# Up projection of a block-algorithm FFN on one core: two channel tiles interleaved, product by product

## Chip, cores, metric

The kernel runs on one core of one Trainium2 chip. The metric is the time of one execution in microseconds (us) of device time, lower is better; where several executions were timed, their median counts. PE is TensorE, DVE is VectorE, ACT is ScalarE, POOL is GpSimd, and SP is the engine whose queue issues nearly all DMAs.

## What is computed

One layer: a token mixer (DeltaNet and grid pooling, not touched here), then a gated FFN with a three-tap convolution over the sequence, all in float32. The change is inside the FFN, for 1024 tokens, D = 1024 and 2816 = 22 x 128 hidden channels:

```python
def conv_glu_ffn(h, w_up, conv_w, w_down):
    gate, up = jnp.split(h @ w_up, 2, axis=-1)
    return (jax.nn.silu(depthwise_conv(gate, conv_w)) * up) @ w_down
```

## The kernel before

Every float32 product is made of three matmuls: each operand is split into a rounded part (`h`) and the rest (`l`), and h·h, l·h and h·l are added up in PSUM. ACT makes the rounded part with a CAST, DVE the rest with a TENSOR_TENSOR.

The up projection works on 22 channel tiles f = 0..21. For one tile, the weights of the gate half and the up half (each 1024 x 128) and the activations (1024 x 1024) are taken as a 2 x 2 block product, which a Strassen-like scheme computes with seven block products instead of eight. Each of the seven is 4 k-blocks x 3 matmuls = 12 matmuls of 128x128 weights and 512 columns. Table `PROD` (line 1463) gives each product its weight block, its activation block and its PSUM bank:

| product p | moving operand | PSUM | what its eviction does |
|---|---|---|---|
| 1 | b11 | pa (X) | ACT copies it to `t1` |
| 6 | T2 | pb (Y) | DVE: gate half 1 = PSUM + t1 (`graw`) |
| 2 | b21 | pa (X, added to 1) | ACT copies it to gate half 0 (`graw`) |
| 7 | T3 | pb (Y, added to 6) | DVE: up half 1 = PSUM + t1 (`upx`) |
| 5 | T1 | pc (Z) | DVE: up half 1 += PSUM |
| 4 | T4 | pb (Y, added to 7) | DVE: up half 0 = PSUM + t1 |
| 3 | B22 | pc (Z, added to 5) | DVE: gate half 1 += PSUM |

Since products share banks, `NEEDS = {2: 1, 7: 6, 4: 7, 3: 5}` (line 1591) makes product 2 wait for the eviction of 1, 7 for that of 6, 4 for that of 7, and 3 for that of 5. `stream_up` (1593) walks through `SEQ` (1465 to 1467); there, tile after tile, the order is 1, 6, 2, 7, 5, 4, 3. The first tiles are special: products of tiles 0 and 1 alternate, and products 1 and 2 of tile 2 are drawn ahead.

The other work of a tile:

- `prep` (1480) loads four weight blocks (tiles `a11`, `a21`, `a22`, `a12`, 256 KB each, eight buffers) and a fifth (`st2`, one buffer), and POOL forms one sum and three differences of them in place.
- `stream_split` (1536) makes the weight halves `wqh` (ACT) and `wql` (DVE) of each product, four buffers each (`NWQ`), in the order of `SEQ`.
- `up_out` (1621) is the eviction. `graw` and `upx` come from one ring of four buffers (`gu`, 1659).
- `gate` (1662) does the convolution on DVE (one TENSOR_SCALAR, two SCALAR_TENSOR_TENSOR), SiLU on ACT, the product with `upx` on DVE and the store `gd`; its result lies in `hf[4 + f % 4]`, where `hf` is a block of eight 128x1024 slots.
- Once per pair of tiles: `sums_S` (1698) makes four sums and differences for the down projection from the two results and stores them (`sd`); `sums_T` (1710) loads two row blocks of `w_down`, makes four differences and stores them (`td`). The two use `hf[0:2]` and `hf[2:4]`. All eleven `sums_T` are done by 972 us.

The engines run their own queues in order. The order in a queue is not that of the Python text: the generators are merged by priority (`Streams`, 128) and the framework then places the instructions. Then follows the down projection (`stream_down`, 1758): 924 matmuls in seven passes.

Of the kernel before, what the change touches and what calls it, by code (L numbers as in the profile page):

```python
# [25 lines left out]
NF = 22  # L26
# [101 lines left out]
class Streams:  # L128
# [7 lines left out]
    def spawn(self, gen, prio):  # L136
        self.active.append([prio, max(self.now, self.clock.end), gen, None, 0])

    def signal(self, name):
        self.events[name] = max(self.now, self.clock.end)  # L140
# [42 lines left out]
def kernel(ctx: ExitStack, tc: tile.TileContext, I, out):  # L183
    nc = tc.nc
    clock = Clock()
    V, S, G, TE, SY = [Engine(clock, n, e) for n, e in (("DVE", nc.vector), ("ACT", nc.scalar), ("POOL", nc.gpsimd),
                                                        ("PE", nc.tensor), ("SP", nc.sync))]
# [1121 lines left out]
    W = {}  # L1309
# [154 lines left out]
            5: ("S1", "T1", "Z"), 6: ("S2", "T2", "Y"), 7: ("S3", "T3", "Y")}  # L1464
    SEQ = [(f, p) for p in (1, 2) for f in (0, 1)] + [(2, 1), (2, 2)]
    SEQ += [(f, p) for p in (6, 7, 5, 4, 3) for f in (0, 1)]
    SEQ += [(f, p) for f in range(2, NF) for p in (1, 6, 2, 7, 5, 4, 3) if f > 2 or p > 2]
    NWQ, NST = 4, 8
    half = (slice(0, 512), slice(512, 1024))
    NJ = NF // 2  # L1470
    CH = [f // 2 + NJ * (f % 2) for f in range(NF)]
    A, wq, up, bank = {}, {}, {}, {}
# [148 lines left out]
    def up_out(f, p, ps):  # L1621

        yield (ps,)
        if p == 1:
            up[f, "t1"] = fT.tile([P, 512], F32, name="t1", bufs=2)
            S.copy(up[f, "t1"], ps)
        else:
            for e in {6: (1,), 5: (7,), 4: (1,), 3: (6,)}.get(p, ()):
                yield f"E{f}{e}"
            if (f, "g") not in up:  # L1630
                yield "FB"
                if f > 1:
                    yield f"g{f - 2}"
            if (f, "g") not in up:
                up[f, "g"] = gu("graw")
                G.memset(up[f, "g"][:, 0:1], 0.0)
                G.memset(up[f, "g"][:, T + 1:T + 2], 0.0)
                up[f, "u"] = gu("upx")
            g, u, t1 = up[f, "g"], up[f, "u"], up[f, "t1"]
            g0, g1 = [g[:, 1 + h.start:1 + h.stop] for h in half]  # L1640
            u0, u1 = [u[:, h] for h in half]
            if p == 2:
                S.copy(g0, ps)
            elif p == 6:
                V.tensor_tensor(g1, ps, t1, ALU.add)
            elif p == 7:
                V.tensor_tensor(u1, ps, t1, ALU.add)
            elif p == 5:
                V.tensor_tensor(u1, ps, u1, ALU.add)
            elif p == 4:  # L1650
                V.tensor_tensor(u0, ps, t1, ALU.add)
            else:
                V.tensor_tensor(g1, ps, g1, ALU.add)
        yield
        signal(f"E{f}{p}")
        if p == 3:
            spawn(gate(f), 3)

    def gu(name):
        return fb.tile([P, T + 2], F32, name=name, tag="gu", bufs=4)  # L1660

    def gate(f):
        yield "TD"
        yield f"E{f}4"
        cw = sm[:, SM_FCONV + 3 * CH[f]:SM_FCONV + 3 * CH[f] + 3]
        rw, u, sg = up[f, "g"], up[f, "u"], W["hf"][:, 4 + f % 4, :]
        V.tensor_scalar(sg, rw[:, 0:T], cw[:, 0:1], None, ALU.mult)
        yield
        V.scalar_tensor_tensor(sg, rw[:, 1:T + 1], cw[:, 1:2], sg, ALU.mult, ALU.add)
        yield  # L1670
        V.scalar_tensor_tensor(sg, rw[:, 2:T + 2], cw[:, 2:3], sg, ALU.mult, ALU.add)
        yield
        S.activation(sg, sg, AF.Silu)
        yield
        V.tensor_tensor(sg, u[:, 0:T], sg, ALU.mult)
        yield
        dma(out=gd[f], in_=sg)
        signal(f"g{f}")
        if f % 2:
            spawn(sums_S(f // 2), 4)  # L1680
        else:
            spawn(sums_T(f // 2), 5)
        yield
# [13 lines left out]

    def sums_S(j):

        (a11, a21), (a12, a22) = [[W["hf"][:, 4 + f % 4, h] for h in half] for f in (2 * j, 2 * j + 1)]  # L1700
        s1, s2, s3, s4 = [blocks(0)[:, i] for i in range(4)]
        for x, y, z, op in ((s1, a21, a22, ALU.add), (s2, s1, a11, ALU.subtract), (s3, a11, a21, ALU.subtract),
                            (s4, a12, s2, ALU.subtract)):
            V.tensor_tensor(x, y, z, op)
            yield
        dma(out=sd[j], in_=blocks(0))
        signal(f"S{j}d")
        yield

    def sums_T(j):  # L1710

        x = blocks(2)
        for i in range(2):
            dma(out=x[:, 2 * i:2 * i + 2], in_=I["w_down"][CH[2 * j + i] * P:(CH[2 * j + i] + 1) * P].rearrange(
                "p (a n) -> p a n", n=512))
        yield (x,)
        b11, b12, b21, b22 = [x[:, i] for i in range(4)]
        for o, y, z in ((b11, b12, b11), (b12, b22, b12), (b22, b22, b11), (b21, b21, b22)):
            V.tensor_tensor(o, y, z, ALU.subtract)
            yield  # L1720
        dma(out=td[j], in_=x)
        signal(f"T{j}d")
        yield
# [218 lines left out]
```

## Time and profile before

| | |
|---|---|
| runs shown | 1374.93, 1380.78, 1381.83 us (median 1380.78) |
| the profiled execution | 1374.41 us, its span 1372.7 us, 1.7 us outside the span |
| PE busy | 1276.5 us (93%) |
| DVE busy | 999.7 us (73%) |
| ACT busy | 624.3 us (45%) |
| POOL busy | 333.8 us (24%) |
| mean granted TensorE clock | 0.973 |

The span is the time from the first to the last instruction. A view "in order of time" has one instruction (or a run of equal ones) per row, with its start, its duration and, in brackets, how long its engine stood idle before it and what ended that. A matmul of 512 columns lasts 0.39 us, but the next one starts 0.23 us after it, so paces are read from start to start.

### The profile page before, as it was taken

The page shows a single profiled execution, that of the slowest core. Times are in us where ns is not written, and L with a number is a line of the kernel's source. Part 1 is how long each engine was busy: PE and PEld are TensorE (multiplying, and loading weights), DVE is VectorE, ACT ScalarE, POOL GpSimd, SP SyncE. Part 2 cuts the span into 40 slices and gives each one's busy share as a digit, 9 for nine tenths or more (in the row PEclk, how much of TensorE's full clock was granted, in tenths as well). Part 3 has the DMA queues.
Part 4 walks back from the last instruction along what each step waited for, and adds up shares of the span by engine and source line. Part 5 has one row for each costly group of instructions (what it writes and reads, how often), then busy time and mean ns, then how long its engine had stood idle before and what let it go on. Part 6 is the DMA issues. An engine that isn't in the chain of part 4 may idle for free. (4 is left out here: it accounts for less than half of the span.)

```text
span 1372.7 us, 23957 instructions
## 1 busy us (share of the span) xinstructions
PE 1276.5 (93%) x8655; PEld 1003.6 (73%) x8655; DVE 999.7 (73%) x2027; ACT 624.3 (45%) x1478; POOL 333.8 (24%) x431
## 2 busy tenths in 40 slices
PE   5888999999999799988979999999999999999997
PEld 1456767777878678766767777787788887888886
DVE  1876655656788688459888998888887769655674
ACT  3555866456676345345443332332333236644540
POOL 0552434141131500012023323332333220000122
PEclk9889999999999999999999999999999999999999
DMA  9513655445462313483224465566433337976561
GB/s 344 193 41 111 204 175 146 141 131 186 120 197 70 101 58 94 151 268 136 110 74 140 166 237 210 213 230 230 154 138 123 116 122 257 308 251 197 187 212 62
DMA packets 145302, 226.55 MB, mean 165 GB/s; under 512 B 53440, under 2 KB 66592, under 8 KB 142368
## 3 DMA queue, kind: packets, MB, share of 16 engines
q1 hardware_dynamic: 144752, 224.61, 48.4%
q8 instruction: 68, 1.11, 0.3%
q14 instruction: 50, 0.41, 0.1%
q10 hardware_dynamic: 432, 0.42, 0.1%
HBM read 164.77 MB, written 60.21 MB: 164 GB/s over the span
## 5 line engine op out<-in xcount | busy, mean ns | idle before, releaser
L123 POOL TENSOR_TENSOR a<-a,a 128x512 f32<-128x512 f32 x88 | 137.9, 1568 | 354.2 <-DMA a<-in_w_up_t 130.1
L123 ACT CAST wqh<-a 128x512 fp32r<-128x512 f32 x132 | 81.1, 620 | 238.9 <-POOL a L123 62.1
L123 DVE TENSOR_TENSOR op<-dst,op 128x512 fp32r<-128x512 f32 x154 | 104.1, 717 | 62.2 <-ACT op L123 61.9
L123 PE MATMUL pa<-h_hi,w_hi 128*128 128x512 f32 x320 | 138.2, 432 | 2.5 <-ACT jk L123 1.2
L123 ACT CAST op<-dst 128x512 fp32r<-128x512 f32 x154 | 89.8, 620 | 99.1 <-PE pc L123 34.2
L123 PE MATMUL pa<-h_hi,w_lo 128*128 128x512 f32 x320 | 129.6, 405 | 1.6 <-DVE w_lo L123 1.6
L123 PE MATMUL pa<-h_lo,w_hi 128*128 128x512 f32 x320 | 130.5, 408 | 0.0
L123 PE MATMUL pc<-op 128*128 128x512 f32 x528 | 121.7, 391 | 1.3 <-DVE graw L123 1.3
L123 PEld LDWEIGHTS pc<-op 128*128 128x128 f32 x528 | 99.1, 188 | 23.2 <-DVE graw L123 1.7
L123 DVE TENSOR_TENSOR wql<-a,wqh 128x512 fp32r<-128x512 f32 x132 | 101.3, 769 | 19.0 <-ACT wqh L123 18.6
L123 DVE TENSOR_TENSOR hf<-hf 128x512 f32<-128x512 f32 x89 | 82.4, 933 | 2.2 <-DMA hf<-in_w_down 1.7
L123 POOL TENSOR_TENSOR hf<-hf,gg 128x512 f32<-128x512 f32 x16 | 21.2, 1350 | 213.7 <-ACT t L123 213.7
L123 PEld LDWEIGHTS pa<-h_hi,w_hi 128*128 128x128 f32 x320 | 61.1, 191 | 16.0 <-issue 2.8
L123 PEld LDWEIGHTS pa<-h_hi,w_lo 128*128 128x128 f32 x320 | 60.9, 190 | 13.9 <-DVE w_lo L123 1.8
L123 DVE SCALAR_TENSOR_TENSOR cv<-raw,sm,cv 128x1024 f32<-128x1024 f32 x48 | 62.3, 1297 | 11.4 <-ACT cv L123 10.9
L123 PEld LDWEIGHTS pa<-h_lo,w_hi 128*128 128x128 f32 x320 | 61.1, 191 | 9.5 <-issue 2.0
L123 DVE SCALAR_TENSOR_TENSOR hf<-graw,sm,hf 128x1024 f32<-128x1024 f32 x44 | 58.5, 1330 | 0.5
L123 PE MATMUL pa<-op 128*128 128x512 f32 x198 | 50.6, 391 | 0.0
L123 PE MATMUL pb<-op 128*128 128x512 f32 x198 | 50.4, 390 | 0.0
L123 ACT ACTIVATE ws<-pc,btg 128x128 f32<-128x128 f32 x80 | 26.9, 367 | 48.6 <-PE pc L123 48.3
L123 DVE TENSOR_TENSOR w_lo<-w_st,w_hi 128x512 fp32r<-128x512 f32 x40 | 27.6, 692 | 26.7 <-ACT w_hi L123 16.9
L123 PE MATMUL pc<-wo_h,mxh 128*128 128x512 f32 x112 | 44.4, 398 | 1.4 <-ACT mxh L123 1.4
(384 smaller groups left out, 3350.1 us busy)
## 6 DMA issues: line engine op xcount, KB each, us to landing
a<-in_w_up_t SPq DMA_DIRECT2D x90, 256.0 KB, 2.7
w_m<-in_wmod SPq DMA_DIRECT2D x64, 256.0 KB, 3.2
hf<-in_w_down SPq DMA_DIRECT2D x22, 512.0 KB, 4.2
td<-hf SPq DMA_DIRECT2D x11, 1024.0 KB, 4.5
gd<-hf SPq DMA_DIRECT2D x22, 512.0 KB, 2.8
sd<-hf SPq DMA_DIRECT2D x11, 1024.0 KB, 3.9
dst<-sd SPq DMA_DIRECT2D x44, 256.0 KB, 5.2
dst<-td SPq DMA_DIRECT2D x44, 256.0 KB, 4.8
```

The source lines that it names most:

```text
L123: return f(*a, **k)
```

## The change

`SEQ` is sorted by a key that sets tile f+1 half a tile behind tile f: from tile 2 on, products of two tiles alternate. So that two tiles can be open at once, the ring `gu` holds `graw` alone from tile 2 on, `upx` moves to `hf[4 + f % 2]`, the gate's result to `hf[6 + f % 2]`, and some waits are renamed: product 7's eviction waits until the gate of tile f-2 is done, and the gate of a tile waits until the `sums_S` of the pair before is stored.

```diff
-    SEQ += [(f, p) for f in range(2, NF) for p in (1, 6, 2, 7, 5, 4, 3) if f > 2 or p > 2]
+    SEQ += [x for _, x in sorted((14 * (f // 2) + 7 * (f % 2) + 2 * i, (f, p)) for f in range(2, NF)
+                                 for i, p in enumerate((1, 6, 2, 7, 5, 4, 3)) if f > 2 or p > 2)]
...
             if (f, "g") not in up:
                 yield "FB"
                 if f > 1:
-                    yield f"g{f - 2}"
+                    yield f"g{f - (2 if f < 4 else 4)}"
...
-                up[f, "u"] = gu("upx")
+            if p == 7 and f > 1:
+                yield f"g{f - 2}"
+            if (f, "u") not in up:
+                up[f, "u"] = gu("upx") if f < 2 else W["hf"][:, 4 + f % 2, :]
...
     def gate(f):
         yield "TD"
         yield f"E{f}4"
+        if f > 1:
+            yield f"S{f // 2 - 1}d"
...
-        rw, u, sg = up[f, "g"], up[f, "u"], W["hf"][:, 4 + f % 4, :]
+        rw, u, sg = up[f, "g"], up[f, "u"], W["hf"][:, 6 + f % 2, :]
...
-        (a11, a21), (a12, a22) = [[W["hf"][:, 4 + f % 4, h] for h in half] for f in (2 * j, 2 * j + 1)]
+        (a11, a21), (a12, a22) = [[W["hf"][:, 6 + i, h] for h in half] for i in range(2)]
```

What this does to the queues is shown at three places. Names have the buffer's number, brackets name the engines whose semaphore is waited for; `h`/`l` after a block's name are its halves.

First PE, in the middle of the stage, around tile 5 (before: banks pb_9525 and pc_9582; now: pb_9476 and pc_9601, and tile 6 is pa_9581 and pb_9620). Only the matmul with which a product begins is shown, eleven more follow each. Before, from product 7 (T3) on:

```order
L123 MATMUL pb_9525<-T3h_8849,wqh_9549 128x512 [waits DVE_49]
...
L123 MATMUL pc_9582<-T1h_8901,wqh_9578 128x512
...
L123 MATMUL pb_9525<-T4h_8945,wqh_9602 128x512 [waits DVE_49,Activation_49]
...
L123 MATMUL pc_9582<-B22h_8968,wqh_9608 128x512 [waits DVE_49,Activation_49]
...
L123 MATMUL pa_9642<-b11h_7749,wqh_9638 128x512 [waits Activation_49]
```

and now:

```order
L123 MATMUL pb_9476<-T3h_8849,wqh_9539 128x512 [waits DVE_49,Activation_49]
...
L123 MATMUL pa_9581<-b11h_7749,wqh_9567 128x512 [waits Activation_49]
...
L123 MATMUL pc_9601<-T1h_8901,wqh_9577 128x512 [waits Activation_49]
...
L123 MATMUL pb_9620<-T2h_8799,wqh_9598 128x512 [waits Activation_49]
...
L123 MATMUL pb_9476<-T4h_8945,wqh_9633 128x512 [waits DVE_49,Activation_49]
...
L123 MATMUL pa_9581<-b21h_7751,wqh_9642 128x512 [waits Activation_49]
...
L123 MATMUL pc_9601<-B22h_8968,wqh_9675 128x512 [waits DVE_49,Activation_49]
```

Between T3 and T4 of a tile stood one product (T1), and now stand three (b11, T1, T2, two of them of the next tile); likewise between T1 and B22.

Second DVE, in the same stretch, with the evictions (they read a pb or pc), the weight splits (wql), the convolution and the sums of hf slots. Before:

```order
L123 TENSOR_TENSOR upx_9544<-pb_9525,t1_9519 128x512
L123 TENSOR_TENSOR wql_9639<-a11_9504,wqh_9638 128x512
L123 TENSOR_TENSOR upx_9544<-pc_9582,upx_9544 128x512
L123 TENSOR_TENSOR wql_9668<-a11_9504,wqh_9667 128x512
L123 TENSOR_TENSOR upx_9544<-pb_9525,t1_9519 128x512
L123 TENSOR_TENSOR wql_9675<-a12_9510,wqh_9674 128x512
L123 TENSOR_TENSOR graw_9541<-pc_9582,graw_9541 128x512
```

and now, from the eviction of tile 5's product 7 on:

```order
L123 TENSOR_TENSOR hf_7753<-pb_9476,t1_9447 128x512
L123 SCALAR_TENSOR_TENSOR hf_7753<-graw_9333,sm_64,hf_7753 128x1024
L123 TENSOR_TENSOR wql_9634<-st2_9573,wqh_9633 128x512
L123 TENSOR_TENSOR hf_7753<-hf_7753 128x512
L123 TENSOR_TENSOR hf_7753<-hf_7753 128x1024
L123 TENSOR_TENSOR wql_9643<-a12_9565,wqh_9642 128x512
L123 TENSOR_TENSOR hf_7753<-hf_7753 128x512
L123 TENSOR_TENSOR hf_7753<-pc_9601,hf_7753 128x512
L123 TENSOR_TENSOR wql_9676<-a12_9384,wqh_9675 128x512
```

The four late evictions of a tile stood side by side, with one split between each two; now they are spread over a longer stretch, with convolution and sums between them. The number of each kind of instruction per tile is the same.

Third DVE again, where the alternation sets in (tile 2: pb_9060, and pc_9123 before, pc_9141 now). Before:

```order
L123 TENSOR_TENSOR graw_9097<-pb_9060,t1_8818 128x512
L123 SCALAR_TENSOR_TENSOR hf_7753<-graw_8807,sm_64,hf_7753 128x1024
L123 TENSOR_TENSOR hf_7753<-upx_8805,hf_7753 128x1024
L123 SCALAR_TENSOR_TENSOR hf_7753<-graw_8807,sm_64,hf_7753 128x1024
L123 TENSOR_TENSOR wql_9106<-st2_9090,wqh_9105 128x512
L123 TENSOR_TENSOR upx_9100<-pb_9060,t1_8818 128x512
```

and now:

```order
L123 TENSOR_TENSOR graw_9097<-pb_9060,t1_8818 128x512
L123 SCALAR_TENSOR_TENSOR hf_7753<-graw_8807,sm_64,hf_7753 128x1024
L123 TENSOR_TENSOR hf_7753<-upx_8805,hf_7753 128x1024
L123 SCALAR_TENSOR_TENSOR hf_7753<-graw_8807,sm_64,hf_7753 128x1024
L123 TENSOR_TENSOR wql_9105<-a22_8928,wqh_9104 128x512
L123 TENSOR_TENSOR hf_7753<-pb_9060,t1_8818 128x512
```

The split at the fifth row was that of product 4 (`st2`); now it is that of product 5 (`a22`), which PE begins earlier.

## Rows read from the trace of the kernel before

**Rows 1.** Page, chain that ended last: share of the span by engine.

```profile
PE 34%; DVE 5%; issue 1%; DMA 1%; ACT 0%; DVEq 0%; ACTq 0%
```

**Rows 2.** Busy time by stretch: us, busy (count) of PE, PEld, DVE, ACT, POOL; clock, DMA share, GB/s.

```profile
792.00:976.00 184.00, 178.39 (x761) 141.96 (x760) 161.50 (x202) 56.36 (x91) 56.54 (x55) 1.00 0.60 221
976.00:1132.00 156.00, 156.00 (x673) 126.26 (x672) 120.98 (x144) 49.95 (x81) 46.82 (x47) 1.00 0.34 123
...
1160.00:1360.00 200.00, 200.00 (x878) 164.57 (x877) 126.18 (x227) 86.94 (x164) 19.97 (x15) 1.00 0.64 213
```

**Rows 3.** PE in order of time: T2 of tile 2, b11 of tiles 4, 13, 21.

```profile
755.45 0.40 PE L123 MATMUL pb<-T2h,wqh 128*128 128x512 f32 x1
...
792.36 0.39 PE L123 MATMUL pa<-b11h,wqh 128*128 128x512 f32 x1
...
975.76 0.39 PE L123 MATMUL pa<-b11h,wqh 128*128 128x512 f32 x1
...
1131.99 0.39 PE L123 MATMUL pa<-b11h,wqh 128*128 128x512 f32 x1
```

**Rows 4.** PE in order of time, starts of four products in a row of tile 17.

```profile
1053.88 0.40 PE L123 MATMUL pa<-b11h,wqh 128*128 128x512 f32 x1
...
1056.61 0.40 PE L123 MATMUL pb<-T2h,wqh 128*128 128x512 f32 x1
...
1059.42 0.39 PE L123 MATMUL pa<-b21h,wqh 128*128 128x512 f32 x1
...
1062.15 0.40 PE L123 MATMUL pb<-T3h,wqh 128*128 128x512 f32 x1
```

**Rows 5.** PE's waits, 755 to 1160 us: total, times, longest.

```profile
PE pb L123 <- DVE upx L123: 6.2, 5, 1.8
PE pc L123 <- DVE graw L123: 1.3, 1, 1.3
```

**Rows 6.** PE in order of time: T1 and T4 of tile 11.

```profile
945.38 0.40 PE L123 MATMUL pc<-T1h,wqh 128*128 128x512 f32 x1
...
950.18 0.47 PE L123 MATMUL pb<-T4h,wqh 128*128 128x512 f32 x1 [1.83 <-DVE upx L123]
```

**Rows 7.** DVE in order of time, ahead of that T4.

```profile
941.07 0.69 DVE L123 TENSOR_TENSOR hf<-hf 128x512 f32<-128x512 f32 x1 [1.31 <-DMA hf<-in_w_down]
...
945.22 4.21 DVE L123 TENSOR_TENSOR hf<-hf 128x512 f32<-128x512 f32 x3
949.35 0.68 DVE L123 TENSOR_TENSOR upx<-pb,t 128x512 f32<-128x512 f32 x1
```

**Rows 8.** DVE in order of time, the split ahead of tile 2's upx.

```profile
764.82 0.68 DVE L123 TENSOR_TENSOR wql<-st,wqh 128x512 fp32r<-128x512 f32 x1
```

**Rows 9.** DVE groups by shape, 792 to 976 us: busy us, mean ns, idle before.

```profile
L123 DVE TENSOR_TENSOR hf<-hf 128x512 f32<-128x512 f32 x55 | 50.0, 918 | 2.0 <-DMA hf<-in_w_down 1.7
L123 DVE TENSOR_TENSOR wql<-a,wqh 128x512 fp32r<-128x512 f32 x55 | 42.8, 778 | 10.8 <-ACT wqh L123 10.8
...
L123 DVE TENSOR_TENSOR hf<-upx,hf 128x1024 f32<-128x1024 f32 x9 | 14.3, 1588 | 0.0
...
L123 DVE TENSOR_TENSOR wql<-st,wqh 128x512 fp32r<-128x512 f32 x9 | 6.2, 684 | 0.0
```

**Rows 10.** POOL group, 792 to 976 us.

```profile
L123 POOL TENSOR_TENSOR a<-a,a 128x512 f32<-128x512 f32 x37 | 56.8, 1535 | 129.6 <-DMA a<-in_w_up_t 46.1 <-DVE wql L123 36.0 <-issue 28.1
```

**Rows 11.** DVE in order of time, one operation before POOL is at work, one beside it.

```profile
1040.80 1.22 DVE L123 TENSOR_TENSOR hf<-upx,hf 128x1024 f32<-128x1024 f32 x1
1041.93 1.78 DVE L123 TENSOR_TENSOR wql<-st,wqh 128x512 fp32r<-128x512 f32 x1
```

**Rows 12.** Page, DMA issues: count, size, median us to landing.

```profile
a<-in_w_up_t SPq DMA_DIRECT2D x90, 256.0 KB, 2.7
...
hf<-in_w_down SPq DMA_DIRECT2D x22, 512.0 KB, 4.2
td<-hf SPq DMA_DIRECT2D x11, 1024.0 KB, 4.5
```

## The prediction

> **What bounds the kernel now.** I begin with the chain that ended last [rows 1]: PE has the largest named share, DVE a small one, and DMA 1%. So I ask next where PE is not full, by stretches [rows 2]. From 1160 us on, in the down projection, PE is busy 200.00 of 200.00 us, and from 976 to 1132 us, in the second half of the up projection, 156.00 of 156.00. There no reordering can win anything. From 792 to 976 us it is busy 178.39 of 184. DVE is busy 161.50 us there, against 120.98 of 156 later, because the `sums_T` differences run in that stretch alone. The granted clock is 1.00 in all of these rows, so the clock takes no part.
>
> Busy time hides part of a loss, so I price the stage by starts. Tiles 13 to 20 run from 975.76 to 1131.99 us [rows 3]: 156.23 / 8 = 19.53 us per tile, the pace without waits. Tiles 4 to 12 run from 792.36 to 975.76: 183.40 us for nine, or 20.38 per tile. Nine at 19.53 are 175.77, so **7.63 us** are lost. From the first product after the change of order (T2 of tile 2, 755.45) to 792.36 are 36.91 us. Without waits, tile 3 costs 19.53, and tile 2, which has its b11 and b21 behind it, 19.53 - 2.73 - 2.73 = 14.07 (b11 lasts from 1053.88 to 1056.61, b21 from 1059.42 to 1062.15 [rows 4]). That makes 33.60, so **3.31 us** are lost. All that the stage has to give is 10.94 us, 0.8% of the time. Half a percent, about what a measurement of this kernel can tell from no change, is 6.9 us.
>
> Who takes it? The waits [rows 5] name DVE's write of `upx`, five times, for a product in pb: that is product 4 (T4), which may start only when 7 (T3) is evicted. The worst case shows how it comes about. T1 of tile 11 starts at 945.38 [rows 6], so T3 ended there. Its eviction starts on DVE only at 949.35 and ends at 950.03 [rows 7], since DVE had first stood idle 1.31 us for a `w_down` load and then had 4.21 us of sums to do. T1, the only product between, ends 2.81 us after 945.38; T4 starts at 950.18, 4.80 after it.
>
> **The change, part by part.**
>
> *Distance between a bank's products.* Three products now stand between 7 and 4, between 5 and 3, and around the others: for T3 to T4 b11, T1 and T2, 2.73 + 2.81 + 2.81 = 8.35 us instead of 2.81. The longest delay of the stretch, 4.80, fits into that with 3.5 to spare, and the shorter ones more easily. For tiles 4 to 12 I therefore take back all 7.63 us. What covers this is DVE's own slack: 161.50 / 184 x 20.38 = 17.9 us per tile, so 1.6 are free at a pace of 19.53. If that is gone, the rivals below price it. What is late next is the weight split: it has four buffers before and after, is made when the product four places ahead has ended, and so leads its use by three products, 8.35 us, unchanged.
>
> *Where the alternation sets in.* In the new order, PE reaches T1 of tile 2 after T2, half of b11, T3 and half of b11: 755.45 + 2.81 + 1.37 + 2.81 + 1.37 = 763.81, and its third matmul, which needs the `wql` split, at 764.27. On DVE, that split stands in the place which the split of product 4 has before, with the same work ahead of it: 764.82 to 765.50 [rows 8]. PE waits 1.2 us there, in the place of the 3.31 lost now. So between 1.2 and 3.31 us stay; I take 2.0, nearer to the one wait that I can place. Gain: 1.3.
>
> *More waits written on PE.* Each product now names ACT at its first matmul and DVE at its third. T2 and b21 do so already and are at full pace (2.81 and 2.73 us [rows 4], b11 with one wait 2.73). Cost 0.
>
> *Moved buffers and new waits on other queues.* Product 7 now waits for the gate two tiles back, and a gate for the sums and the store of the pair before. The two gates and the sums are on DVE itself, in this order in its queue, so they add no wait between engines; the stores were issued a tile or more earlier. Cost 0, at most one load as waited for once [rows 7], 1.3 us.
>
> *SP and POOL.* The same DMAs are issued, weight loads among them behind the `w_down` loads that wait for a `td` store; 4.5 us [rows 12] is what a weight load can be held up by, and it lands in 2.7, while the first split from it stands a tile, 19.53 us, later. Cost 0. POOL forms A6 after the split of product 1 in 1.54 us [rows 10], and the split that needs it is now two products away instead of one. Cost 0.
>
> *The hand-over to the down projection.* PE waits 1.3 us for the last `graw` [rows 5]. The last products of tile 21 still stand alone, but gate 20 and its sums fall three products later, among the operand splits of the down projection. Between -1.3 and +1.8 us (a wait like the longest of the stage [rows 5]); I take 0, since the eviction stands behind about as many splits as before.
>
> **Sum.** 7.63 + 1.3 = 8.9 us. The profiled execution took 1374.41 us, so with the change 1365.5. But it lies at the low end of the runs shown, 6.4 us under their median of 1380.78. On that median the sum is **1371.9 us**, my forecast.
>
> **A rule that speaks against it.** Operations of DVE with both inputs in SBUF take longer while POOL runs: 1.78 us for a split [rows 11] that takes 0.684 undisturbed [rows 9]. On average, splits stand at 0.778 us, `hf<-hf` at 0.918 and the gate's product `hf<-upx` at 1.588 [rows 9]; undisturbed they are 0.684 [rows 9], 0.69 [rows 7] and 1.22 [rows 11]. That makes 55 x 0.094 + 55 x 0.228 + 9 x 0.368 = 21 us in some nine tiles, 2.3 per tile.
>
> The Trainium skill (SBUF — State Buffer, "Who interferes with whom") says that a DVE instruction with two SBUF inputs contends with a GpSimd instruction that reads SBUF, and that the second to issue blocks until the first is done. The trace agrees with the rule (1.78 against 0.684). By it, what the new order puts beside POOL's subtractions decides DVE's slack; by the average row the sum stays 8.9 us, by the rule's worst case it would be rival B's or A's.
>
> **Rivals.**
>
> *A, slower: DVE becomes the bound in tiles 4 to 12.* POOL does 37 subtractions in nine tiles [rows 10], 4.1 per tile. If each held up one DVE operation by 1.78 - 0.68 = 1.1 us, that were 4.5 per tile instead of 2.3: 17.9 + 2.2 = 20.1. With one wait for a `w_down` load like the 1.31 us [rows 7] in every tile, where now 2.0 us come in the whole stretch [rows 9], it is 21.2. PE then waits in every product for its split: 9 x (21.2 - 20.38) = 7.4 us lost, 1388 us. It decides from 20.38 per tile on. For it: a `td` store and a load take 4.5 + 4.2 = 8.7 us [rows 12] and the differences of the next pair stand in the middle of DVE's queue. Against: the same kinds and numbers of operations, 1.6 us of slack, and both worst cases at once.
>
> *B, hardly faster.* POOL's worst case alone, 20.1 per tile: 9 x (20.38 - 20.1) = 2.5 us won, plus 1.3: 1377 us. For it: evictions and splits no longer stand together, and sums with two SBUF inputs come between them. Against: 4.1 conflicts per tile, all at full length.
>
> *C, it doesn't do what it says.* DVE is late as a whole rather than in spots, and the wait moves from `upx` to the splits: 1380.8 us. For it: DVE is 88% busy [rows 2]. Against: DVE itself stands idle 10.8 us ahead of its splits, for ACT's half of them [rows 9], so it is not late throughout.
>
> **How the numbers follow.** I give the forecast 0.66, B 0.21, C 0.08, A 0.05. If the whole 10.94 and the hand-over's 1.3 go, it is 1368.6 us; a median as low as the profiled execution would bring the forecast to 1365.5. B and C reach to 1380.8. So the range is 1364 to 1380.8, leaving out A and a little on either side. Faster by over 0.5% (under 1373.9) is the forecast without its weakest part, 0.63; within 0.5%: B, C and that part, 0.32; slower: A, 0.05.
>
> **What would show it.** Right: no wait of a pb or pc product for `upx` or `hf` longer than a few tenths from tile 4 on; tiles 4 to 12 at 19.5 to 19.6 us each; some 1.2 us before T1 of tile 2; PE over 99% busy from 792 to 976 us; stretches before 755 us unchanged. Wrong: waits for `wql` in many products (A, B); DVE over 95% busy there, or its mean `hf<-hf` well above 918 ns (the rule's worst case); a wait of 3 us or more at the hand-over.

## The result and the profile after

The changed kernel takes 1364.07 us (median of 6 runs, 1361.48 to 1366.20) against 1381.30 for the kernel before (6 runs, 1374.93 to 1383.21): 0.9893 times, 95% interval 0.9871 to 0.9914. A second comparison, on a fresh set of runs (e5 below), gives 0.9918, 0.9889 to 0.9947: medians of 1366.81 (9 runs) and 1378.35 us (28 runs). The gap is 17.2 us the first time and 11.5 the second. The two profiles lie only 8.2 us apart (1374.41 and 1366.20). Which of the three is the gain of the change can be read from starts in the trace.

PE in order of time in the changed kernel: T2 of tile 2, where the order begins to differ, then b11 of tiles 4, 13 and 21 (compare [rows 3]):

```profile
758.64 0.40 PE L123 MATMUL pb<-T2h,wqh 128*128 128x512 f32 x1
...
784.41 0.40 PE L123 MATMUL pa<-b11h,wqh 128*128 128x512 f32 x1
...
960.03 0.40 PE L123 MATMUL pa<-b11h,wqh 128*128 128x512 f32 x1
...
1116.13 0.40 PE L123 MATMUL pa<-b11h,wqh 128*128 128x512 f32 x1
```

From tile 4's b11 to tile 13's are 175.62 us, 19.51 per tile, where it was 183.40: 7.78 us come back. From 13 to 21 nothing changes (156.10 against 156.23). The whole stage, from T2 of tile 2 to the end of the last up product of tile 21 (nine operand matmuls of the down projection already stand within it, in both kernels), takes 398.13 us before (755.45 to 1153.58) and 388.02 after (758.64 to 1146.66). Right behind it, 1.27 us of wait for `graw` [rows 5] are gone. **The stage gains 10.1 + 1.3 = 11.4 us.** It begins 3.2 us later in this profile, after the same instructions; that is why the profiles show 8.2.

PE's waits in the changed kernel, 755 to 1160 us (total, times, longest; compare [rows 5]), and its busy time by stretch (compare [rows 2]):

```profile
PE pb L123 <- DVE graw L123: 0.4, 1, 0.4
PE pb L123 <- DVE hf L123: 0.3, 1, 0.3
```

```profile
792.00:976.00 184.00, 184.00 (x793) 148.99 (x793) 172.64 (x208) 58.64 (x94) 66.58 (x56) 1.00 0.62 225
976.00:1132.00 156.00, 156.00 (x673) 126.33 (x672) 123.29 (x149) 52.12 (x85) 46.19 (x41) 1.00 0.38 130
```

PE is full where the sums of the down weights are formed, and DVE is now busy 172.64 of 184 us, 18.3 per tile of 19.51: 1.2 us are free in each. In the chain that ended last, the shares (PE 72% now, 34% before [rows 1]) can't be set side by side: the rows of before add up to 41%, so that chain covers less than half of the span.

The operations of DVE have changed places with each other. Groups of DVE by shape, 792 to 976 us, in the changed kernel (busy us, mean ns, idle before; compare [rows 9]):

```profile
L123 DVE TENSOR_TENSOR wql<-a,wqh 128x512 fp32r<-128x512 f32 x59 | 50.4, 856 | 3.5 <-ACT wqh L123 3.4
L123 DVE TENSOR_TENSOR hf<-hf 128x512 f32<-128x512 f32 x56 | 41.8, 747 | 0.3
L123 DVE SCALAR_TENSOR_TENSOR hf<-graw,sm,hf 128x1024 f32<-128x1024 f32 x18 | 29.0, 1610 | 0.3
L123 DVE TENSOR_TENSOR wql<-st,wqh 128x512 fp32r<-128x512 f32 x9 | 15.0, 1662 | 0.0
L123 DVE TENSOR_TENSOR hf<-pb,t 128x512 f32<-128x512 f32 x19 | 13.0, 683 | 0.0
L123 DVE TENSOR_TENSOR hf<-hf 128x1024 f32<-128x1024 f32 x9 | 10.9, 1213 | 0.5 <-ACT hf L123 0.5
```

The differences `hf<-hf` fall from 918 to 747 ns and the gate's product from 1588 to 1213, while the split of product 4 (`wql<-st`) rises from 684 to 1662 and the convolution's steps from 1282 to 1610. Which operation is drawn out depends on where it falls. Eight of the nine splits of product 4 now run while a sum of POOL is under way and take 1.78 to 1.79 us; the ninth does not, and takes 0.68. In order of time, one of the eight and the ninth:

```profile
903.86 1.79 DVE L123 TENSOR_TENSOR wql<-st,wqh 128x512 fp32r<-128x512 f32 x1
...
963.94 0.68 DVE L123 TENSOR_TENSOR wql<-st,wqh 128x512 fp32r<-128x512 f32 x1
```

### The profile page after: what moved, and what is told of

Same layout as the page of the kernel before. It is cut to its first block, busy times and chain, and to the rows that moved or that the text cites. A ratio compares the mean times of both kernels' runs of the same rounds, so it can differ in the third digit from the quotient of the medians.

```text
span 1364.5 us, 23950 instructions
## 1 busy us (share of the span) xinstructions
PE 1276.8 (94%) x8655; PEld 1006.3 (74%) x8655; DVE 1008.1 (74%) x2027; ACT 624.9 (46%) x1478; POOL 338.3 (25%) x431
## 4 chain that ended last, share of the span: by engine, by line
PE 72%; DVE 13%; DMA 6%; ACT 3%; issue 3%; POOL 2%; SPq 0%; DVEq 0%; ACTq 0%; POOLq 0%
PE pa L123 27%; PE pc L123 23%; PE pb L123 22%; DVE hf L123 2%; DMA w_m<-in_wmod 1%; DMA w_mod<-in_wmod 1%; DVE x L123 1%; DVE gtmp L123 1%; POOL sX L123 1%; DVE rs_a L123 1%; POOL stmp L123 1%; DVE wql L123 1%; DVE yrs L123 1%; DMA wo_st<-in_w_out 1%; DMA sc<-blk_x 1%
## 5 line engine op out<-in xcount | busy, mean ns | idle before, releaser
L123 POOL TENSOR_TENSOR a<-a,a 128x512 f32<-128x512 f32 x88 | 143.4, 1630 | 320.4 <-DVE wql L123 158.5
L123 DVE TENSOR_TENSOR wql<-a,wqh 128x512 fp32r<-128x512 f32 x132 | 104.6, 795 | 17.2 <-ACT wqh L123 17.1
L123 DVE TENSOR_TENSOR hf<-hf 128x512 f32<-128x512 f32 (+1 forms) x109 | 92.3, 853 | 7.1 <-ACT hf L123 6.7
L123 DVE SCALAR_TENSOR_TENSOR hf<-graw,sm,hf 128x1024 f32<-128x1024 f32 x44 | 71.3, 1621 | 0.7
L123 DVE SCALAR_TENSOR_TENSOR cv<-raw,sm,cv 128x1024 f32<-128x1024 f32 x48 | 62.6, 1305 | 11.4 <-ACT cv L123 10.8
L123 ACT ACTIVATE hf<-hf 128x1024 f32<-128x1024 f32 x22 | 23.4, 1062 | 58.0 <-DVE hf L123 58.0
```

Of the source, the lines that this page charges most:

```text
L123: return f(*a, **k)
```

## Experiments

In the table, the stage is the stretch defined above, and "tiles 4 to 12" runs from b11 of tile 4 to b11 of tile 13. The last column compares with runs of the kernel before from the same chip (95% interval; their medians are 1378.35 to 1381.30). Two entries need a correction to be compared: in e3, going back to the old order puts 36 matmuls more between the two b11 (792 instead of 756, 8.4 us at 0.23), so 180.4 us are to be set beside the others; in e8 the stage ends with T4 at 1157.52 and the nine operand matmuls follow it, so their 2.05 us are added.

| kernel | stage, us | tiles 4 to 12 | median, us | ratio to before |
|---|---|---|---|---|
| before | 398.13 | 183.40 | 1381.30 | |
| the change | 388.02 | 175.62 | 1364.07 | 0.9893 (0.9871 to 0.9914) |
| e1 before again | 398.27 | 184.17 | 1377.29, one run | |
| e5 the change again | 388.07 | 175.62 | 1366.81 | 0.9918 (0.9889 to 0.9947) |
| e2 buffers alone | 398.75 | 184.41 | 1378.10 | 0.9994 (0.9977 to 1.0011) |
| e3 old order from tile 12 on | 392.38 | 188.81 (180.4) | 1368.68 | 0.9929 (0.9902 to 0.9956) |
| e4 before, no differences | 391.60 | 176.90 | 1371.55 | 0.9954 (0.9934 to 0.9973) |
| e8 spread inside a tile | 402.30 | 188.47 | 1378.58 | 0.9997 (0.9979 to 1.0016) |
| e10 the change, DVE +0.75 us per tile | 390.46 | 178.16 | 1368.51 | 0.9927 (0.9901 to 0.9952) |
| e6 the change, DVE +1.5 us per tile | 396.55 | 183.02 | 1373.59 | 0.9963 (0.9945 to 0.9980) |
| e7 before, DVE +1.5 us per tile | 411.26 | 188.48 | 1387.77 | 1.0066 (1.0041 to 1.0091) |
| e9 as e6, without POOL's sums | 388.42 | 175.62 | 1357.71 | 0.9856 (0.9804 to 0.9908) |
| e11 before, without POOL's sums | 387.46 | 175.92 | 1354.46 | 0.9844 (0.9813 to 0.9875) |
| e12 the change, first POOL sums later | 388.19 | 175.62 | 1359.90 | 0.9862 (0.9835 to 0.9889) |

### Which of the three gaps is the gain (e1, e5)

No edit: the kernel before and the changed kernel, once more.

> The kernel before, unchanged, profiled once more. Its one profile so far took 1374.41 us, the median of its runs is 1381.3; the profile of the changed kernel took 1366.2, the median of its runs is 1364.07. Profile against profile 8.2 us, median against median 17.2. Theory 1: the waits of the alternating stage differ from execution to execution of the kernel before, and its profile was a lucky one; in a second one of some 1380 us the stage from T2 of tile 2 to the first operand product of the down projection takes 402 to 407 us, against 398.1 in the first and 388.0 in the changed kernel. Theory 2: the spread comes from the stretches before 755 us (there the changed kernel's profile is 3.2 us later than that of before, with the same instructions); then the stage takes 397.5 to 399 us again, and the second profile differs before 755 us.

> The changed kernel unchanged, beside a fresh set of runs of before. The stage from T2 of tile 2 to the first operand product of the down projection took 398.1 and 398.3 us in two executions of before, with 1.2 to 1.3 us of wait right behind it, and 388.0 with none in one of the change: 11.4 us. The instructions of the 755 us ahead of the stage are the same and their end moved by up to 3.2 us between executions. Theory 1 (the gain is that of the stage alone, and the 17 us between the first medians hold some 6 us of that scatter): the stage takes 387.8 to 388.3 us again, and the medians lie 10 to 13 us apart. Theory 2 (something outside the stage gains too): medians 15 us or more apart.

The first product of the stage starts at 758.23 us in e1 (755.45 in [rows 3]). PE's waits in its stage:

```profile
PE pb L123 <- DVE upx L123: 6.2, 6, 2.0
```

The stage of e1 takes 398.27 us, that of e5 388.07: both repeat to 0.15 us, and the waits stand before the same products again, one more of 0.5 us in tile 9 among them. What moves is its start: 755.45, 758.23, 758.64 and 764.46 us in four executions whose PE runs the same products up to there. So theory 2 of e1 and theory 1 of e5 hold: the gain is the 11.4 us of the stage, and 17.2 and 8.2 are the same gain with the scatter of the earlier stages in it. This scatter goes with the granted clock of TensorE: of 78 runs of the kernel before, the 19 with a mean clock of 0.975 or more have a median of 1374.9 us, the 15 with 0.969 or less 1381.0. In the stage the clock is 1.00 in both kernels. Whether the clock makes the scatter was not tested.

### Order or buffers (e2)

```diff
-    SEQ += [x for _, x in sorted((14 * (f // 2) + 7 * (f % 2) + 2 * i, (f, p)) ...
+    SEQ += [(f, p) for f in range(2, NF) for p in (1, 6, 2, 7, 5, 4, 3) if f > 2 or p > 2]
```

> The order of before with the buffers and waits of the change. Theory 1 (distance in PE's order does it): the waits of product 4 for the eviction of 7 stay, stage 396 to 400 us as in the profile of before (398.1), time within 3 us of the kernel before. Theory 2 (the buffers do it: the up tile and the gate's result in other memory, so that gate and evictions wait less): stage near 388 us, time 10 us or more under before.

The waits stay, now under the name of the new buffer (PE's waits, 755 to 1160 us):

```profile
PE pb L123 <- DVE hf L123: 6.6, 6, 1.8
```

398.75 us against 398.13 and 398.27: in the stage the buffers and their new waits bring nothing and cost nothing. The order does it. The hand-over is another matter: behind the stage PE runs on without a wait here too, in the old order:

```profile
1156.25 19.04 PE L123 MATMUL pc<-op 128*128 128x512 f32 x82
```

So the order is shown to bring the 10.1 us of the stage; that it brings the 1.3 at the hand-over is not shown.

### Where the gain is made (e3)

```diff
-    for f in range(2, NF) ...   (alternating)
+    for f in range(2, 12) ...   (alternating), then range(12, NF) tile by tile
```

> The change, but the tiles from 12 on in the order of before. Theory 1 (the gain is made where the sums of the down weights are formed, tiles 2 to 12): all of the gain but the 1.3 us at the hand-over stays, plus at most one wait in tile 12 where the order goes back, 0.4 us; time 0 to 2 us over the changed kernel. Theory 2 (in typical executions of before the later tiles wait too, and that is the difference between 8.2 and 17.2 us): time 5 us or more over the changed kernel, and waits for the up tile after 980 us.

Neither held. From tile 13 on nothing is lost (156.21 us for eight tiles), as theory 1 has it, but going back costs 4.4 us in the stage, not 0.4. PE and then DVE, in order of time, at that point:

```profile
960.05 0.40 PE L123 MATMUL pc<-T1h,wqh 128*128 128x512 f32 x1
...
964.92 0.48 PE L123 MATMUL pb<-T4h,wqh 128*128 128x512 f32 x1 [1.91 <-DVE hf L123]
...
966.37 0.63 PE L123 MATMUL pb<-T4h,wql 128*128 128x512 f32 x1
966.79 0.63 PE L123 MATMUL pb<-T4h,wqh 128*128 128x512 f32 x1
```

```profile
957.61 4.63 DVE L123 TENSOR_TENSOR hf<-hf 128x1024 f32<-128x1024 f32 x3
962.17 0.68 DVE L123 TENSOR_TENSOR wql<-a,wqh 128x512 fp32r<-128x512 f32 x1
962.77 1.41 DVE L123 TENSOR_TENSOR hf<-hf 128x512 f32<-128x512 f32 x2
964.10 0.68 DVE L123 TENSOR_TENSOR hf<-pb,t 128x512 f32<-128x512 f32 x1
```

Tile 12 is the first whose product 4 has only one product in front of it again, and it pays at once: T3 ends at 960.05, its eviction starts 4.05 us later, behind a run of three operations of 4.63 us, a split and two differences. The wait of 1.91 us and one of 0.81 ahead of this T3 make 2.7. Most of the rest is clock: behind the wait, eight matmuls of T4 start 0.42 to 0.43 us apart instead of 0.23, 1.6 us more, and from 964.9 to 969.3 us the granted clock is 0.62, that is, for part of that time at the lower of its two levels (1.2 GHz, not 2.4); in the kernel before it stays at 1.00 behind waits of up to 1.83 us. Late spots are there in the alternating order too, they are only not seen: in the changed kernel T2 of tile 4 ends at 792.75 and DVE comes to its eviction at 795.83, 3.1 us later, and is done 4.6 us before T3 needs the bank at 801.11.

### What makes the eviction late (e4, e8, e11)

e4 takes the four differences of `sums_T` away, e8 changes the order inside a tile, e11 takes POOL's work away. All three start from the kernel before.

```diff
 e4, sums_T
-        for o, y, z in ((b11, b12, b11), (b12, b22, b12), (b22, b22, b11), (b21, b21, b22)):
-            V.tensor_tensor(o, y, z, ALU.subtract)
-            yield
 e8
-    for p in (1, 6, 2, 7, 5, 4, 3)
+    for p in (1, 6, 5, 7, 2, 3, 4)      (and the eviction of 5 writes u1, that of 7 adds to it)
 e11, prep
-        G.tensor_tensor(q["22"], q["21"], q["22"], ALU.add)      (and the three differences after it)
```

> The kernel before with the four differences of the down weights left out in every pair (the loads and stores stay; the output is then wrong by what is left out: the down projection multiplies the weight blocks themselves). VectorE loses 44 operations of 0.92 us, 40 us in tiles 2 to 12. Theory 1 (these differences stand ahead of the eviction of 7 and make product 4 wait): from tile 4 on no wait for the up tile over 0.3 us, tiles 4 to 12 at 19.5 to 19.6 us; of the 10.9 us that the stage loses at least 7.6 come back, time 7 to 11 us under before. Theory 2 (the eviction is late through the gate and the weight splits, and the differences only happen to stand there): half of the waits or more stay, time within 4 us of before.

> The kernel before with another order inside a tile and no new buffers: products 1, 6, 5, 7, 2, 3, 4, so that two products stand between 7 and 4 (5.5 us instead of 2.8) and two between 5 and 3, while 6 and 7 keep one between; the eviction of 5 writes the tile first and that of 7 adds to it. Theory 1 (the distance from 7 to 4 is what was short; the longest delay was 4.8 us): no wait for the up tile of more than 0.3 us from tile 4 on, stage at most 391 us, time 7 to 10 us under before. Theory 2 (VectorE is late once per tile, and whichever product has only one in front of it waits): the waits move to product 7, for the eviction of 6, and the stage stays at 394 us or more, time within 5 us of before.

> The kernel before, with GpSimd's four subtractions and sums of weight blocks per tile left out (the products take the unsummed blocks, so the output is wrong by them). It tells how much of the late evictions in before is contention. In tile 11 three differences ahead of the eviction of 7 took 4.21 us together; at 0.69 each they are 2.1, and the delay of product 4 would shrink from 4.8 us to 2.7, under the 2.81 that the one product between lasts. Theory 1 (the late spots are made of operations drawn out beside GpSimd): no wait for the up tile over 0.3 us from tile 4 on, stage 389 to 392.5 us, like the 391.6 without the differences. Theory 2 (the eviction stands too far back in VectorE's queue, whatever its operations last): half of the waits stay, stage 394 us or more.

PE's waits, 755 to 1160 us, in e4:

```profile
PE pb L123 <- DVE upx L123: 2.2, 2, 1.3
```

In tiles 4 to 12, 6.5 of 7.6 us come back (176.90 us); what stays is the loss ahead of tile 4, as in before, and one wait in tile 4. The median is 7.2 us under before, the low end of what theory 1 gave. So far the differences looked like the cause.

e8 shows that one longer distance isn't enough. PE's waits, 755 to 1165 us:

```profile
PE pb L123 <- DVE graw L123: 8.9, 9, 2.6
```

Product 4 waits for nothing any more, but now product 7 waits for the eviction of 6, nine times. Theory 2: DVE is late once per tile, and the product that still has only one in front of it pays. Not all of its loss is waiting: behind the waits of 2.6 and 1.9 us (803 and 909 us) the matmuls of product 7 start 0.43 us apart, at a granted clock of 0.51 (803.4 to 806.5 us) and 0.55 (908.5 to 912.3), 1.4 and 1.7 us more. With the same work in it, its stage is 4.2 us longer than that of before, and 1.3 less are lost behind it; the medians don't show this (0.9997, 0.9979 to 1.0016).

e11 gives the cause below that one. DVE groups by shape and busy time by stretch, 792 to 976 us:

```profile
L123 DVE TENSOR_TENSOR wql<-a,wqh 128x512 fp32r<-128x512 f32 x57 | 39.0, 684 | 0.6
L123 DVE TENSOR_TENSOR hf<-hf 128x512 f32<-128x512 f32 x49 | 33.1, 687 | 0.3
...
L123 DVE TENSOR_TENSOR hf<-upx,hf 128x1024 f32<-128x1024 f32 x9 | 11.0, 1218 | 0.0
```

```profile
792.00:976.00 184.00, 184.00 (x793) 148.72 (x792) 142.23 (x201) 58.29 (x93) 1.20 (x18) 1.00 0.61 213
```

In the **old** order, with all differences in place, PE waits nowhere in the stage, neither in tiles 4 to 12 (175.92 us) nor ahead of them (33.58 us from T2 of tile 2 to b11 of tile 4, against 36.91); the one wait left is that for `graw` at the hand-over, 1.85 us. Theory 1, and more than it gave. Every operation with two inputs in SBUF now takes its undisturbed time (differences 687 ns against 918, the gate's product 1218 against 1588). So the evictions were late because POOL's weight sums run beside DVE's queue; the differences stood in it, but at 0.69 us each they would have done no harm. One more thing goes with POOL's sums: ACT's waits for them, and with these nearly all of the 10.8 us in which DVE stood idle for ACT's half of the splits [rows 9] (0.6 us idle are left in e11). At the late spots themselves DVE does not stand idle for ACT. Its queue in before, in order of time, ahead of the wait of tile 4 (T3 ends at 803.46, T1 at 806.27):

```profile
802.28 1.81 DVE L123 TENSOR_TENSOR wql<-a,wqh 128x512 fp32r<-128x512 f32 x1
804.01 2.98 DVE L123 TENSOR_TENSOR hf<-hf 128x512 f32<-128x512 f32 x3
806.91 0.68 DVE L123 TENSOR_TENSOR upx<-pb,t 128x512 f32<-128x512 f32 x1
```

These four operations take 4.63 us from the first start to the eviction's; undisturbed, at 0.69 each, 2.8. The eviction would start 1.8 us earlier, at some 805.1, and be done before T1 ends. At the other three waits of tiles 4 to 12 for the eviction of 7 (tiles 5, 7 and 11) it is the same: the operations ahead are longer than undisturbed by 2.2, 2.3 and 2.1 us, and PE waits 0.81, 0.63 and 1.83. In tile 7:

```profile
863.56 1.82 DVE L123 TENSOR_TENSOR wql<-a,wqh 128x512 fp32r<-128x512 f32 x1
865.30 3.23 DVE L123 TENSOR_TENSOR hf<-hf 128x512 f32<-128x512 f32 x3
```

So contention alone accounts for these four waits, 4.6 of the 7.6 us. How the rest of e11's gain divides between it and ACT's waits is not separated.

### How much slack the new order has (e6, e7, e10, e9)

An operation that changes no value is issued again in `gate`; e10 has one more, e6 and e7 two, e9 two but none of POOL's sums.

```diff
-        V.tensor_scalar(sg, rw[:, 0:T], cw[:, 0:1], None, ALU.mult)
+        for _ in range(3):
+            V.tensor_scalar(sg, rw[:, 0:T], cw[:, 0:1], None, ALU.mult)
```

> The change, with the gate's first VectorE operation (0.745 us, one input from memory, the same result) issued three times in each tile: 1.49 us of VectorE more per tile. From 792 to 976 us VectorE is busy 172.6 of 184 us in the changed kernel, 18.3 of 19.53 per tile, so 1.2 are free. Theory 1 (the new order hides lateness until VectorE is full on average): tiles 4 to 12 become 0.3 us longer each, 2 to 4 us in all, and tiles 13 on stay at 19.53. Theory 2 (the distance of three products is barely enough, a later eviction shows at once): 0.7 to 1.5 us per tile, 7 to 14 in tiles 4 to 12.

> The same two extra operations per tile in the kernel before. VectorE is busy 17.9 us per tile of 20.38 there, so 2.5 are free on average. Theory 1 (a product with one product between waits for lateness of its eviction however much is free on average): tiles 4 to 12 lose another 0.7 to 1.5 us each, 6 to 13 us in all, more than the changed kernel does under the same load, and the later tiles may begin to wait. Theory 2 (average load decides): at most 2 us more.

> The changed kernel with one extra VectorE operation per tile (0.745 us) instead of two. With two, tiles 4 to 12 became some 0.75 us longer, by waits for the split of product 3 in every other tile. Theory 1 (VectorE full on average is the threshold; 1.2 us were free): 18.3 + 0.75 = 19.1 under 19.53, so at most 1 us is lost in all, stage 388 to 389.5 us. Theory 2 (the splits' lead is used up by single late spots, in proportion to the load): half of the loss with two, stage 391.5 to 393 us.

> The changed kernel with the two extra VectorE operations per tile (as in the run before, whose stage took 396.55 us with VectorE busy 179.43 of 184 us), and GpSimd's four subtractions and sums of weight blocks per tile left out (the products then take the unsummed blocks, so the output is wrong by them). In the changed kernel splits stand at 856 and 1662 ns, the gate's scalar_tensor_tensor at 1610, against 684 and some 1240 beside an idle GpSimd: 59 x 0.17 + 56 x 0.06 + 18 x 0.37 + 9 x 0.98 = 29 us in 9.4 tiles, 3.1 per tile. Theory 1 (that is contention with GpSimd): the means fall to 0.68 to 0.70 for splits and differences and under 1.3 us for the gate, VectorE is under 17.5 us per tile in spite of the load, the waits for the split go, and the stage takes 388 to 389.5 us. Theory 2 (the long operations come from something else, such as the DMA writes into the same memory): the means stay over 0.8 for the splits and the stage at 394 us or more.

Busy time by stretch in e6, and PE's waits, 755 to 1165 us:

```profile
792.00:976.00 184.00, 179.29 (x762) 142.05 (x761) 179.43 (x217) 54.55 (x92) 63.10 (x53) 1.00 0.61 217
```

```profile
PE pc L123 <- DVE wql L123: 5.3, 5, 1.2
```

The 1.5 us cost 7.4 in tiles 4 to 12 (183.02), the size that theory 2 named. But no eviction is waited for: PE waits for the split of product 3 in every other tile, with DVE busy 97.5% of the time. That is the forecast's "late next", and it comes as soon as DVE is full.

e7 loses 13.1 us in the stage, more than e6's 8.5, but not as theory 1 said: 7.8 of them fall ahead of tile 4 (where PE waits 3.7 us for ACT's half of a split and 2.1 for an eviction, and the next twelve matmuls run at a granted clock of 0.50), and in tiles 4 to 12 it loses 5.1, under the 6 that theory 1 gave and less than e6. In tiles 4 to 12 the alternating kernel still does a tile in 20.3 us (183.02 / 9) against 20.9 (188.48 / 9).

e10 lies between its theories: 2.5 us, all of them in tiles 9 to 12 (19.83, 20.12, 20.50 and 20.14 us, the others 19.51 to 19.52). The gate's product has gone from 1213 ns to

```profile
L123 DVE TENSOR_TENSOR hf<-hf 128x1024 f32<-128x1024 f32 x10 | 22.4, 2237 | 1.1 <-ACT hf L123 1.1
```

in e10, while the split of product 4 has gone from 1662 to 1170. DVE as a whole is busy 18.9 us per tile (175.78 of 184, at 19.8), within what theory 1 gave; what has moved is which operations meet POOL. The waits are short ones, for two evictions and one split (0.3 to 0.4 us each). Why they begin only in tile 9 is not shown.

In e9, with twice e10's load and no sums on POOL, the wait for the split is gone. DVE groups by shape and busy time by stretch, 792 to 976 us:

```profile
L123 DVE TENSOR_TENSOR wql<-a,wqh 128x512 fp32r<-128x512 f32 x56 | 38.4, 685 | 7.7 <-ACT wqh L123 7.6
...
L123 DVE SCALAR_TENSOR_TENSOR hf<-graw,sm,hf 128x1024 f32<-128x1024 f32 x18 | 23.0, 1279 | 0.0
...
L123 DVE TENSOR_TENSOR wql<-st,wqh 128x512 fp32r<-128x512 f32 x10 | 6.9, 685 | 0.0
```

```profile
792.00:976.00 184.00, 184.00 (x793) 149.02 (x793) 156.99 (x223) 58.80 (x94) 1.20 (x18) 1.00 0.63 219
```

156.99 us in 9.43 tiles (184 / 19.51) are 16.6 per tile in spite of 1.5 more work: theory 1. Against these undisturbed means, contention costs the changed kernel 59 x 0.171 + 56 x 0.061 + 18 x 0.331 + 9 x 0.977 = 28 us in the stretch, 3.0 per tile. The same sum for before, with its own means, is 21 us in 9.0 tiles, 2.3 per tile.

### The first sums on POOL held back (e12)

e9 and e11 also reach the up projection sooner: from the first pc product of the output projection to the first b11 are 91.5 and 89.9 us, where the kernels with POOL's sums take 98.0 to 100.6. POOL in order of time in the changed kernel, and PE's waits from 600 to 700 us:

```profile
614.16 4.03 POOL L123 TENSOR_TENSOR a<-a,a 128x512 f32<-128x512 f32 x3 [73.01 <-DVE rs_h L123]
619.51 2.96 POOL L123 TENSOR_TENSOR a<-a,a 128x512 f32<-128x512 f32 x2 [1.31 <-DMA a<-in_w_up_t]
624.92 4.47 POOL L123 TENSOR_TENSOR a<-a,a 128x512 f32<-128x512 f32 x3 [2.45 <-DVE wql L123]
```

```profile
PE pb L123 <- DVE xr L123: 6.0, 3, 4.6
PE pc L123 <- DVE mxl L123: 2.3, 1, 2.3
```

The sums of tiles 0 and 1 are made there, beside splits that PE waits for, and are needed only by the first product 6, at 721 us. e12 holds them back.

```diff
 prep, tiles 0 and 1: the load of a22 is left out of the loop, and then
+        if f < 2:
+            yield "H2"
+            G.tensor_tensor(late[:, 0, 0:2], W["hf"][:, 7, 256:258], W["hf"][:, 7, 256:258], ALU.add)
+            dma(out=late, in_=src["22"])      (late is the buffer of a22)
         yield (q["21"], q["22"])
```

> The changed kernel, with GpSimd's sums of weight blocks for tiles 0 and 1 held back: their fourth load is issued only after a token tile of the output projection is normalised (a two-column GpSimd operation on that tile writes into the buffer first), so that the eight subtractions and sums, at 614 to 629 us in the changed kernel, come after some 655 us. From the first product of the output projection in bank pc to the first b11 product are 98.0 to 100.6 us in the runs with these operations and 89.9 and 91.5 in the two without any of GpSimd's sums. Theory 1 (this difference is the contention of these eight operations with the splits and residual sums that PE waits for from 612 to 631 us): with the operations later the stretch takes 91 to 95 us, the stage 387.8 to 388.5 us as before, and the time is 4 to 8 us under the changed kernel, 15 to 19 under the kernel before. Theory 2 (contention moves along: at 655 us and later it makes the same work late): 97.5 us or more in the stretch, time within 2 us of the changed kernel. Theory 3 (the sums come too late for the split of the first product 6): waits of PE for its split at some 720 us.

POOL in order of time in e12, and PE's waits from 600 to 700 us:

```profile
653.38 11.10 POOL L123 TENSOR_TENSOR a<-a,a 128x512 f32<-128x512 f32 x8 [3.17 <-issue]
```

```profile
PE pb L123 <- DVE yss L123: 4.8, 2, 2.6
PE pb L123 <- DVE xr L123: 2.5, 2, 1.6
```

The stretch takes 93.8 us (603.48 to 697.28), the stage 388.19, the median 1359.90. Theory 1, with a part of theory 2: the waits for `mxl` are gone and those for `xr` shorter, but there are 4.8 us of waits for `yss`, 3.8 more than in the changed kernel: 2.6 at 659 us, beside the sums, and 2.2 at 672, behind them. It is 4 to 7 us under the two medians of the changed kernel. The two were not timed against each other; two of its six runs (1356.95 to 1362.08) lie above the lowest of the fifteen of the changed kernel.

## Why the prediction was right, and where it was off

**Direction and mechanism.** Right, as far as it went: the distance takes the waits back. That the measured 1364.07 us lies in the range (1364 to 1380.8) is luck, it is 0.07 us inside; the gain that the trace shows, 11.4 us, is 2.5 more than the 8.9 forecast. The rest of the gap between 1371.9 and 1364.07 goes with the scatter of the stages ahead: in the second comparison, 1378.35 - 8.9 = 1369.5 was to be expected, and 1366.81 came, 2.6 under it.

**Distance between a bank's products.** 7.63 us to be taken back in tiles 4 to 12; 7.78 came. That the longest delay fits into three products holds, and e8 and e3 show that all distances have to be long: with one short one left the loss goes there.

**Where the alternation sets in.** The wait of 1.2 us before T1 of tile 2 did not come, and this is the term that was mis-sized: 2.0 of 3.31 us were to stay, 0.4 did. PE reached T1 8.98 us after the start of the stage, not 8.36 (it had waited 0.4 for an eviction ahead of T3), and its split was there sooner. DVE in order of time, the same gate product before, and then that product and the split in the changed kernel:

```profile
761.40 2.31 DVE L123 TENSOR_TENSOR hf<-upx,hf 128x1024 f32<-128x1024 f32 x1
```

```profile
764.40 1.21 DVE L123 TENSOR_TENSOR hf<-upx,hf 128x1024 f32<-128x1024 f32 x1
...
766.73 0.68 DVE L123 TENSOR_TENSOR wql<-a,wqh 128x512 fp32r<-128x512 f32 x1
```

The split starts 8.09 us after 758.64; in before the split in its place starts 9.37 after 755.45 [rows 8]. The step took the work ahead of it at the durations of before. But the gate product and the convolution step ahead of it took 2.31 and 2.39 us there, beside two sums of POOL (759.09 to 762.61), and 1.21 and 1.27 here, beside none.

**The hand-over.** 0 was taken between -1.3 and +1.8; it is -1.3. The reason given (about as many splits stand ahead of the eviction) doesn't hold: between the last two evictions DVE makes three splits before and six now. What counts is that in before it stood idle among them for ACT's half, and now works without a break. DVE in order of time, before and after:

```profile
1154.42 1.30 DVE L123 TENSOR_TENSOR op<-dst,op 128x512 fp32r<-128x512 f32 x2 [1.95 <-ACT op L123]
1155.64 0.69 DVE L123 TENSOR_TENSOR graw<-pc,graw 128x512 f32<-128x512 f32 x1
```

```profile
1144.03 3.70 DVE L123 TENSOR_TENSOR op<-dst,op 128x512 fp32r<-128x512 f32 x6
1147.64 0.69 DVE L123 TENSOR_TENSOR graw<-pc,graw 128x512 f32<-128x512 f32 x1
```

The last eviction now ends 1.7 us after its product (1146.66 to 1148.33) instead of 2.8 (1153.58 to 1156.33). e2 has no wait there either, in the old order and with three splits, but with only 0.31 us of idle for ACT; so this term may be owed to the buffers, and what shortens ACT's lag is not shown. A wait of 0.3 us before T4 of tile 21 is new. 7.8 + 2.9 - 0.3 + 1.3 = 11.7, the 11.4 within the roundings of the paces.

**Waits on PE, moved buffers, SP and POOL at 0.** Right in the stage: e2 shows the buffers and their waits alone at 398.75 us, within 0.6 us of before, and in the changed kernel, with the new waits on PE, a tile takes 19.51 us and PE waits for no load and no sum of POOL.

**The rule that speaks against it.** It held as a fact and failed as an objection. The Trainium skill (SBUF — State Buffer, "Who interferes with whom") has a DVE instruction with two SBUF inputs contend with a GpSimd one that reads SBUF; e9 and e11 agree: without POOL's sums, splits stand at 684 to 685 ns and differences at 686 to 687, and the means of the operations with one input in PSUM (683 ns in the changed kernel, 691 in e9) don't move with POOL. The new order does raise this cost, from 2.3 to 3.0 us per tile, but not to the worst case of 4.5, on which rivals A and B rested; DVE stays at 18.3 us per tile. What the prediction missed is that POOL's sums are also the cause of the loss that the change takes back: e11 gets there in the old order. It put the lateness down to the load, the sums and their place in the queue, although its own worst case held the hint: three differences in 4.21 us [rows 7], 2.1 undisturbed.

**Rivals.** C (the wait moves to the splits) did not come, but e6 shows it 1.5 us of DVE work per tile away; at 0.75 (e10) PE waits for one split and two evictions. The free 1.6 us per tile of the forecast were 1.2.

**What would show it.** No wait over a few tenths from tile 4 on, tiles at 19.51, PE 100% busy from 792 to 976 us, DVE under 95%: all came. The wait before T1 of tile 2 didn't. The stretches before 755 us have the same instructions as before, but their times vary by up to 9 us between executions.

## What to carry to other kernels

Where a product waits for the eviction of the one before in its bank, put enough other products between *all* such pairs to cover the other engine's latest spot, not its average; one short distance left brings waits back (e3, e8). Before that, ask why the spot is late: here a third engine stretched the operations in the queue, and leaving its work out shortens the stage as much (387.5 us) as hiding the effect does (388.0). (e11 leaves the sums out and computes something else; it tells the cause, and is no version to use.) Price the gain from a stage whose starts repeat, not from medians alone: here the stage repeats to 0.15 us while whole runs of one kernel scatter by 10 and more.

## What was not expected of the hardware

The waits of the stage come at the same products in both executions of a kernel (but for one of 0.5 us in e1), each within 0.7 us and their sum within 0.2, although the stage starts 2.8 us later in the one execution of before and 5.8 in that of the change; they belong to the program, not to chance. And contention is no fixed sum per operation: one extra operation with a single SBUF input took the gate's product from 1213 to 2237 ns and the split of product 4 from 1662 to 1170 (e10), because it moved what meets POOL's sums. Last, a wait can cost PE more than its length: behind waits of 1.9 us in e3 and e8 the next matmuls ran at a lower granted clock (0.62 and 0.55) and took 1.6 and 1.7 us more, while behind those of 1.8 and 2.0 in the two executions of before the clock stayed at 1.00.
